# Strassen's weight sums: adding transfers on GpSimd's queue instead of VectorE additions

## The chip, the cores and the metric

The kernel runs on one core of a Trainium2 chip. A core has TensorE (matmuls; PE in the profile), VectorE (DVE), ScalarE (ACT), GpSimd (POOL) and SyncE (SP, which here only issues transfers), each with its own queue, and 16 DMA engines. The metric is the device time of one execution in microseconds. Before the change the median of 3 runs was 1128.04 us (1127.5 to 1130.51).

## The reference

Two layers over x of 512 tokens by 1024 features, all in float32. Layer 0 mixes tokens by differential attention, layer 1 by a short gated convolution; both are followed by a dense MLP:

```
def sq_relu_mlp(x, w_up, w_down):
    return jnp.square(jax.nn.relu(x @ w_up)) @ w_down

for i in range(DEPTH):
    h = rmsnorm(x, norm_mixer_pre[i])
    m = diff_attention(h, ...) if i % 2 == 0 else short_conv(h, ...)
    x = x + rmsnorm(m, norm_mixer_post[i])
    h = rmsnorm(x, norm_mlp_pre[i])
    x = x + rmsnorm(sq_relu_mlp(h, w_up[i], w_down[i]), norm_mlp_post[i])
```

w_up is 1024 x 4096, w_down 4096 x 1024.

## The kernel before, in words

**Products in three matmuls.** Every float32 operand is split into a rounded part hi and the rest lo. `split` (L199) writes hi on ScalarE (L200) and lo = operand - hi on VectorE (L201). A product of two operands is then three matmuls, hi hi, hi lo and lo hi (`mm3`, L67 to L69).

**Up projection.** The weights of the 32 feature tiles come one by one (512 KB each, `raw_up`), are split, and give 24 matmuls each into one PSUM bank. Banks 6 and 7 take turns (in a layer's first six tiles, banks 0 to 5). `squared` empties the bank on ScalarE: Relu (L674) into a scratch tile F, then Square (L675). Two feature tiles make a pair; from its F come the splits ua and ub, with differences made on VectorE (L699 to L701) in between.

**Down projection.** 28 of the 32 rows of w_down tiles are multiplied in Strassen's form (seven products instead of eight): pair p holds rows 2p and 2p + 1, each cut into two halves of 512 columns. Call the four pieces r0, r1 (row 2p) and r2, r3 (row 2p + 1). They lie in one buffer `rawd` with a fifth slot r4. The products need these operands of the weights: A = (r0, r2); E = (r0 + r1, r4) with r4 = r0 + r1 + r3; D = r3; and G = (r1 + r3, r4 + r2). So the sums are made in place: L222 adds r1 and r3 to r0 and r1 (128x1024), L223 makes r4 (128x512), L229 makes the new r2 (128x512). All three are on VectorE. A is split from the buffer before r0 and r2 are overwritten; E, D and G after their sums.

**Groups.** Two pairs (GROUP = 2) are one group: 7 groups in each layer, 14 in all, 28 buffers. A group's 84 matmuls go in the order A, E, G, D, G into banks 0 to 5; between them VectorE adds finished banks to `acc` (L724). Between two groups stand four up products (six before the last group of a layer, none before the first but the layer's first six). Four rows at the end of each layer (`raw_dn`) go without Strassen's form.

**What sets the order.** `order` lists the units: ..., up tiles, A p, A p+1, E p, E p+1, D, G p, G p+1, up tiles, ... `use` asks for the splits of a unit and of the four after it (LEAD), as far as the six slots for hi and lo (SLOTS) allow: a unit's slot is that of the unit six places before. Thus a group's A and E are split during the up products ahead of it. There are two `rawd` buffers (RAWDS), so that the next group's loads wait for the splits of G. Loads are issued by SP in the order of their use. A scheduler then fixes each engine's order; engines work their queues in order, and an instruction that waits holds those behind it.

Of the kernel before, what the change touches and what calls it, by code (L numbers as in the profile page):

```python
# [13 lines left out]
ALU = mybir.AluOpType  # L14
# [14 lines left out]
GROUP = 2  # L29
# [12 lines left out]
def trunk(ctx: ExitStack, tc: tile.TileContext, x, xT, w_qk, w_v, w_o, w_in, w_out,  # L42
          w_up, w_down, rows, cols, lam4, rope, out):
    nc = tc.nc
    PE, ACT, DVE, POOL = nc.tensor, nc.scalar, nc.vector, nc.gpsimd
# [53 lines left out]
    groups = [list(range(g, g + GROUP)) for g in range(0, PAIRED // 2, GROUP)]  # L99
# [32 lines left out]
    def loaded_by(u):  # L132

        n, i = u
        if n[0] in "AEG" and n[1:].isdigit():
            return [("rawd", n[1], i)]
        if n[0] == "D":
            return [("rawd", n[1], p) for p in groups[i]]
        return [("raw", n, i)]
# [8 lines left out]
    units, raws, xts = [], {}, []  # L148
# [15 lines left out]
    def issue():  # L164
        while n_issued[0] < len(loads):
            ld = loads[n_issued[0]]
            tag, n, i = ld
            live = in_flight[tag] = [x for x in in_flight[tag] if last_use[x] >= len(units)]
            if len(live) >= limit[tag] or tag not in allowed:
                return  # L170
            if tag == "rawd" and any(n_done[0] <= j < first_use[ld] for j in ring["rawd"]):
                return
            live.append(ld)
            first = n_issued[0] == 0
            n_issued[0] += 1
            if tag == "rawd":

                raw = raws[ld] = wp.tile([P, 5, 512], F32, tag=tag, name=f"rawd_{n}_{i}", bufs=RAWDS)
                for k in range(2):
                    nc.sync.dma_start(raw[:, 2 * k:2 * k + 2, :].rearrange("p a b -> p (a b)"), w_down[int(n), 2 * i + k])  # L180
                continue
            if n == "v":
                xt = t512(ap, f"xt_{i}", "a", RAWS)
                xts.append(xt)
            src = w_qk[2 * i + "qk".index(n)] if n in "qk" else source[n][i]
            raw = raws[ld] = wp.tile([P, 1024], F32, tag="raw", name=f"raw_{n}_{i}", bufs=RAWS)
            for p in range(2 if first else 1):
                if n == "v":
                    s = pieces(512, first)[p]
                    nc.sync.dma_start(xt[:, s], xT[i][:, s])  # L190
                s = pieces(1024, first)[p]
                nc.sync.dma_start(raw[:, s], src[:, s])
                if n == "v" and i == p == 0:
                    nc.sync.dma_start(col, cols)

    def pieces(n, cut):
        return (slice(0, n // 2), slice(n // 2, n)) if cut else (slice(0, n),)

    def split(hi, lo, src, on_dve=False):  # L199
        (DVE.tensor_copy if on_dve else ACT.copy)(hi, src)  # L200
        DVE.tensor_tensor(lo, src, hi.bitcast(F32), op=ALU.subtract)  # L201

    def make(j):
        n, i = order[j]
        if where[j][0] == "w":
            hi = wp.tile([P, 1024], F32R, tag="whi", name=f"hi_{n}_{i}")
            lo = wp.tile([P, 1024], F32R, tag="wlo", name=f"lo_{n}_{i}")
        else:
            both = wp.tile([P, 2, 1024], F32R, tag="rawd", name=f"both_{n}_{i}", bufs=RAWDS)
            hi, lo = both[:, 0, :], both[:, 1, :]  # L210
        parts = [raws[ld] for ld in loaded_by((n, i))]
        if loaded_by((n, i))[0][0] == "raw":
            if n == "v":
                split_xT(i)
            for s in pieces(1024, j < 2 or n in "qk"):
                split(hi[:, s], lo[:, s], parts[0][:, s], j < 1)
        else:
            r, (h2, l2) = parts[0], (t.rearrange("p (a b) -> p a b", a=2) for t in (hi, lo))
            if n[0] == "A":
                split(h2, l2, r[:, 0:4:2, :])  # L220
            if n[0] == "E":
                DVE.tensor_tensor(r[:, 0:2, :], r[:, 0:2, :], r[:, 1:4:2, :], op=ALU.add)  # L222
                DVE.tensor_tensor(r[:, 4, :], r[:, 0, :], r[:, 3, :], op=ALU.add)  # L223
                split(h2, l2, r[:, 0:5:4, :])
            if n[0] == "D":
                for k, p in enumerate(parts):
                    split(h2[:, k, :], l2[:, k, :], p[:, 3, :])
            if n[0] == "G":
                DVE.tensor_tensor(r[:, 2, :], r[:, 4, :], r[:, 2, :], op=ALU.add)  # L229
                split(h2, l2, r[:, 1:3, :])  # L230
        units.append((hi, lo))

    def split_to(j):
        for j_ in range(len(units), min(j + 1, len(order))):
            if where[j_][1] >= n_done[0]:
                break
            make(j_)
            issue()
# [33 lines left out]
    def split_xT(kt):  # L272

        g = g_pre[:, kt:kt + 1]
        for s in pieces(T, kt == 0):
            hi, lo = hT[0][:, kt, s], hT[1][:, kt, s]
            ACT.activation(hi, xts[kt][:, s], AF.Copy, scale=g)
            DVE.scalar_tensor_tensor(lo, xts[kt][:, s], g, hi.bitcast(F32), op0=ALU.mult, op1=ALU.subtract)
# [5 lines left out]
    def t512(pool, name, tag, bufs):  # L284
        return pool.tile([P, 512], F32, tag=tag, name=name, bufs=bufs)

    issue()
    ones = ap.tile([P, P], F32, name="ones", bufs=1)
    DVE.memset(ones, 1.0)
# [47 lines left out]
    for b in range(NB):  # L337
        for n in range(2):
            o = v_sb[:, b, n * 512:(n + 1) * 512]
# [240 lines left out]
    pool_of_chunks[:] = [(up_, CHUNKS[0])] * CHUNKS[0] + [(late, CHUNKS[1])] * CHUNKS[1]  # L580
    allowed.append("rawd")
    issue()
    x_sb = late.tile([P, NB, D], F32, name="x_sb", bufs=1)

# [301 lines left out]
```

## Time and profile before

| | |
|---|---|
| median of 3 runs | 1128.04 us |
| the profiled execution | 1127.7 us |
| its span, first to last instruction | 1125.9 us |
| TensorE busy | 1101.4 us, 98% |
| VectorE busy | 823.4 us, 73% |
| ScalarE busy | 545.2 us, 48% |
| GpSimd busy | 99.0 us, 9% |
| DMA moved | 114.31 MB, 102 GB/s in the mean |

The profile is of one execution. Busy time is the share in which an engine's instructions run. A timeline row is: start in us from the span's start, duration in us, engine, line, operation, out<-in with shapes, count of instructions that the row joins; in square brackets the idle time of the engine before it and what ended it. Matmuls are pipelined: a row's duration is longer than the distance to the next.

### The profile page before, as it was taken

The page shows a single profiled execution, that of the slowest core. Times are in us where ns is not written, and L with a number is a line of the kernel's source. Part 1 is how long each engine was busy: PE and PEld are TensorE (multiplying, and loading weights), DVE is VectorE, ACT ScalarE, POOL GpSimd, SP SyncE. Part 2 cuts the span into 40 slices and gives each one's busy share as a digit, 9 for nine tenths or more (in the row PEclk, how much of TensorE's full clock was granted, in tenths as well). Part 3 has the DMA queues.
Part 4 walks back from the last instruction along what each step waited for, and adds up shares of the span by engine and source line. Part 5 has one row for each costly group of instructions (what it writes and reads, how often), then busy time and mean ns, then how long its engine had stood idle before and what let it go on. Part 6 is the DMA issues. An engine that isn't in the chain of part 4 may idle for free.

```text
span 1125.9 us, 14245 instructions
## 1 busy us (share of the span) xinstructions
PE 1101.4 (98%) x5404; PEld 915.7 (81%) x5404; DVE 823.4 (73%) x1251; ACT 545.2 (48%) x925; POOL 99.0 (9%) x108
## 2 busy tenths in 40 slices
PE   9999999999999999999998999999999999999997
PEld 7876677778988888888887988888988888888886
DVE  5589999756788779778688544436587887797766
ACT  5546566544664544554545332224375445445532
POOL 0144455211000000000001000000000000000000
PEclk9999999999999999999998999999999999999999
DMA  8611111036134214315042322213231242242202
GB/s 311 217 57 57 57 57 53 23 113 225 38 113 150 86 65 150 104 46 188 1 150 96 130 94 94 95 55 115 93 133 64 103 150 86 65 150 99 88 20 75
DMA packets 33044, 114.31 MB, mean 102 GB/s; under 512 B 3792, under 2 KB 4432, under 8 KB 32976
## 3 DMA queue, kind: packets, MB, share of 16 engines
q1 hardware_dynamic: 32976, 113.41, 29.3%
q8 instruction: 42, 0.69, 0.2%
q14 instruction: 26, 0.21, 0.1%
HBM read 111.30 MB, written 2.10 MB: 101 GB/s over the span
## 4 chain that ended last, share of the span: by engine, by line
PE 80%; DVE 13%; POOL 3%; issue 2%; ACT 1%; DMA 1%; SPq 0%; POOLq 0%; DVEq 0%; ACTq 0%
PE bank L69 24%; PE bank L67 24%; PE bank L68 24%; PE bank L309 2%; PE pair L309 2%; DVE nm L475 2%; DVE a L500 1%; POOL t_q L375 1%; DVE k L392 1%; DVE x_sb L612 1%; DVE pair L474 1%; PE bank L629 1%; PE pair L67 1%; PE pair L69 1%; PE pair L68 1%
## 5 line engine op out<-in xcount | busy, mean ns | idle before, releaser
L67 PE MATMUL bank<-hT_hi,hi_up 128*128 128x512 f32 (+1 forms) x608 | 216.5, 356 | 0.0
L69 PE MATMUL bank<-hT_hi,lo_up 128*128 128x512 f32 (+1 forms) x608 | 216.2, 356 | 0.0
L68 PE MATMUL bank<-hT_lo,hi_up 128*128 128x512 f32 (+1 forms) x608 | 216.1, 355 | 0.0
L68 PEld LDWEIGHTS bank<-hT_lo,hi_up 128*128 128x128 f32 x608 | 114.9, 189 | 16.3
L67 PEld LDWEIGHTS bank<-hT_hi,hi_up 128*128 128x128 f32 x608 | 114.9, 189 | 16.3
L69 PEld LDWEIGHTS bank<-hT_hi,lo_up 128*128 128x128 f32 x608 | 114.9, 189 | 16.2
L724 DVE TENSOR_TENSOR acc<-acc,bank 128x512 f32<-128x512 f32 x180 | 116.5, 679 | 4.4 <-PE bank L69 4.4
L200 ACT CAST hi_up<-raw_up 128x1024 fp32r<-128x1024 f32 x64 | 67.2, 1054 | 86.9 <-PE bank L69 76.4
L201 DVE TENSOR_TENSOR lo_up<-raw_up,hi_up 128x1024 fp32r<-128x1024 f32 x64 | 76.7, 1217 | 8.8 <-ACT hi_up L200 8.8
L201 DVE TENSOR_TENSOR lo_G<-rawd,hi_G 128x1024 fp32r<-128x1024 f32 x28 | 34.2, 1220 | 44.2 <-ACT hi_G L200 44.2
L68 PE MATMUL bank<-hT_lo,hi_ci 128*128 128x512 f32 (+1 forms) x176 | 62.9, 358 | 1.8 <-DVE b_m L601 1.8
L67 PE MATMUL bank<-hT_hi,hi_ci 128*128 128x512 f32 (+1 forms) x176 | 62.8, 357 | 0.9 <-ACT hT_hi L632 0.8
L69 PE MATMUL bank<-hT_hi,lo_ci 128*128 128x512 f32 (+1 forms) x176 | 62.8, 357 | 0.0
L674 ACT ACTIVATE F<-bank 128x512 f32<-128x512 f32 x64 | 37.6, 593 | 45.3 <-PE bank L69 35.8
L200 ACT CAST hi_G<-rawd 128x1024 fp32r<-128x1024 f32 x28 | 29.5, 1053 | 46.0 <-PE bank L68 30.8
L201 DVE TENSOR_TENSOR lo_E<-rawd,hi_E 128x1024 fp32r<-128x1024 f32 x28 | 34.2, 1220 | 23.4 <-ACT hi_E L200 23.4
L201 DVE TENSOR_TENSOR lo_A<-rawd,hi_A 128x1024 fp32r<-128x1024 f32 x28 | 33.5, 1219 | 19.5 <-ACT hi_A L200 19.5
L200 ACT CAST hi_E<-rawd 128x1024 fp32r<-128x1024 f32 x28 | 29.3, 1048 | 34.8 <-PE bank L68 33.4
L200 ACT CAST hi_A<-rawd 128x1024 fp32r<-128x1024 f32 x28 | 29.5, 1053 | 30.4 <-PE bank L68 21.7
L67 PE MATMUL bank<-hi_A,ua_hi 128*128 128x512 f32 x112 | 44.0, 393 | 0.0
L68 PE MATMUL bank<-lo_A,ua_hi 128*128 128x512 f32 x112 | 43.6, 390 | 0.0
L67 PE MATMUL bank<-hi_E,ub_hi 128*128 128x512 f32 x112 | 43.6, 389 | 0.0
(300 smaller groups left out, 2661.7 us busy)
## 6 DMA issues: line engine op xcount, KB each, us to landing
raw_up<-in_w_up SPq DMA_DIRECT2D x64, 512.0 KB, 4.2
rawd<-in_w_down SPq DMA_DIRECT2D x56, 512.0 KB, 4.5
raw_ci<-in_w_in SPq DMA_DIRECT2D x24, 512.0 KB, 3.4
raw_q<-in_w_qk SPq DMA_DIRECT2D x8, 512.0 KB, 4.4
raw_k<-in_w_qk SPq DMA_DIRECT2D x8, 512.0 KB, 3.8
raw_wo<-in_w_o SPq DMA_DIRECT2D x8, 512.0 KB, 3.5
raw_dn<-in_w_down SPq DMA_DIRECT2D x8, 512.0 KB, 3.5
raw_wc<-in_w_out SPq DMA_DIRECT2D x8, 512.0 KB, 3.4
```

The source lines that it names most:

```text
L67: PE.matmul(o, lhsT=a[0], rhs=b[0], start=start, stop=False, skip_group_check=more)
L68: PE.matmul(o, lhsT=a[0], rhs=b[1], start=False, stop=False, skip_group_check=more)
L69: PE.matmul(o, lhsT=a[1], rhs=b[0], start=False, stop=stop, skip_group_check=more)
L200: (DVE.tensor_copy if on_dve else ACT.copy)(hi, src)
L201: DVE.tensor_tensor(lo, src, hi.bitcast(F32), op=ALU.subtract)
L309: PE.matmul(banks[2 * b + n], lhsT=hT[ai][:, kt, b * P:(b + 1) * P], rhs=w[bi][:, n * 512:(n + 1) * 512], start=kt == 0 and ai + bi == 0, ...
L375: POOL.tensor_tensor(t1, t1, sw, op=ALU.add)
L392: DVE.tensor_tensor(tiles[c][other], t1[mine], tiles[c][mine].bitcast(F32), op=ALU.subtract)
L474: DVE.tensor_tensor(dgl, dgl, mask.unsqueeze(1).broadcast_to([P, 2, P]), op=ALU.add)
L475: DVE.tensor_reduce(nm, s[:, :, :w], axis=AX.X, op=ALU.max, negate=True)
L674: ACT.activation(dst, o, AF.Relu)
L724: DVE.tensor_tensor(a, a, o[t], op=op)
```

## The change

The three sums leave VectorE. Each buffer gets one more plain load: r3 is also loaded into the slot r4. When A's split is emitted, `sums` emits adding transfers on GpSimd's queue (`POOL.dma_start` with `accum_op`): the transfer adds its source to what stands at the destination. First r1 and r3 are added, from DRAM, to r0 and r1 (512 KB). With the last pair of a group come two for each of its buffers, within SBUF: r0 is added to r4, and r4 to r2 (256 KB each).

```
@@ -178,6 +178,7 @@
                 raw = raws[ld] = wp.tile([P, 5, 512], F32, tag=tag, name=f"rawd_{n}_{i}", bufs=RAWDS)
                 for k in range(2):
                     nc.sync.dma_start(raw[:, 2 * k:2 * k + 2, :].rearrange("p a b -> p (a b)"), w_down[int(n), 2 * i + k])
+                nc.sync.dma_start(raw[:, 4, :], w_down[int(n), 2 * i + 1][:, 512:1024])
                 continue
@@ -199,6 +200,20 @@
+    def plus(o, a):
+        POOL.dma_start(o, a, accum_op=ALU.add)
+
+    def sums(l, p):
+        r = raws["rawd", l, p]
+        plus(r[:, 0:2, :], w_down[int(l), 2 * p:2 * p + 2, :, 512:1024].rearrange("k p c -> p k c"))
+        pq = [raws["rawd", l, x] for x in groups[p // GROUP]] if p % GROUP == GROUP - 1 else []
+        for r in pq:
+            plus(r[:, 4, :], r[:, 0, :])
+        for r in pq:
+            plus(r[:, 2, :], r[:, 4, :])
@@ -218,15 +233,13 @@
             if n[0] == "A":
                 split(h2, l2, r[:, 0:4:2, :])
+                sums(n[1], i)
             if n[0] == "E":
-                DVE.tensor_tensor(r[:, 0:2, :], r[:, 0:2, :], r[:, 1:4:2, :], op=ALU.add)
-                DVE.tensor_tensor(r[:, 4, :], r[:, 0, :], r[:, 3, :], op=ALU.add)
                 split(h2, l2, r[:, 0:5:4, :])
             if n[0] == "G":
-                DVE.tensor_tensor(r[:, 2, :], r[:, 4, :], r[:, 2, :], op=ALU.add)
                 split(h2, l2, r[:, 1:3, :])
```

GpSimd's queue at the first two groups of layer 0, in the kernel after (`rawd_0` to `rawd_3` are the buffers of pairs 0 to 3; in brackets the semaphores waited for: DMAHW of SP's transfers, DMASW of GpSimd's own):

```order
L74 TENSOR_TENSOR rb_wo_2564<-rb_wo_2564,mhalf 128x1 [waits DVE_49,Pool_49]
L205 DMA rawd_0_2589<-in_w_down 128x2x512 [waits DMAHW5_49,DVE_49]
L205 DMA rawd_1_2593<-in_w_down 128x2x512 [waits DMAHW1_49,DVE_49]
L205 DMA rawd_0_2589<-rawd_0_2589 128x512 [waits DMAHW7_49,DMASW0_49]
L205 DMA rawd_1_2593<-rawd_1_2593 128x512 [waits DMAHW3_49,DMASW1_49]
L205 DMA rawd_0_2589<-rawd_0_2589 128x512 [waits DMAHW6_49,DMASW2_49]
L205 DMA rawd_1_2593<-rawd_1_2593 128x512 [waits DMAHW2_49,DMASW3_49]
L205 DMA rawd_2_3039<-in_w_down 128x2x512 [waits DMAHW0_49,DMASW4_49,DVE_49]
```

Before, the instruction behind `rb_wo` on this queue belonged to the layer's end; now 42 adding transfers for each layer stand between them. The add into r4 waits for the first add into the same buffer, the add into r2 for the add into r4.

VectorE between the splits of A and E in a group of layer 0 (pairs 4 and 5), before:

```order
L201 TENSOR_TENSOR lo_A_4_3418<-rawd_4_3329,hi_A_4_3417 128x1024
L201 TENSOR_TENSOR lo_A_5_3449<-rawd_5_3332,hi_A_5_3448 128x1024
L222 TENSOR_TENSOR rawd_4_3329<-rawd_4_3329 128x1024
L222 TENSOR_TENSOR rawd_5_3332<-rawd_5_3332 128x1024
L223 TENSOR_TENSOR rawd_4_3329<-rawd_4_3329 128x512
L223 TENSOR_TENSOR rawd_5_3332<-rawd_5_3332 128x512
L229 TENSOR_TENSOR rawd_4_3329<-rawd_4_3329 128x512
L229 TENSOR_TENSOR rawd_5_3332<-rawd_5_3332 128x512
L201 TENSOR_TENSOR lo_E_4_3490<-rawd_4_3329,hi_E_4_3489 128x1024
```

and after (the same lines are now L202):

```order
L202 TENSOR_TENSOR lo_A_4_3424<-rawd_4_3333,hi_A_4_3423 128x1024
L202 TENSOR_TENSOR lo_A_5_3456<-rawd_5_3337,hi_A_5_3455 128x1024
L202 TENSOR_TENSOR lo_E_4_3502<-rawd_4_3333,hi_E_4_3501 128x1024
L202 TENSOR_TENSOR lo_E_5_3533<-rawd_5_3337,hi_E_5_3532 128x1024
L712 TENSOR_TENSOR F_5_3452<-F_5_3452 128x512
```

The six sums are gone, and nothing stands between the two splits.

ScalarE in the first group of layer 0 (`F_1`, `ua_1` belong to the second pair of up tiles), before:

```order
L200 CAST ua_0_hi<-F_0_2793 128x768
L200 CAST hi_E_0_2905<-rawd_0_2589 128x1024
L200 CAST ub_0_hi<-F_0_2793 128x1024
L200 CAST hi_E_1_2938<-rawd_1_2592 128x1024
L200 CAST hi_D_0_2981<-rawd_0_2589 128x512
L674 ACTIVATE F_1_2861<-bank_2577 128x2x256
L674 ACTIVATE F_1_2861<-bank_2578 128x2x256
L675 ACTIVATE F_1_2861<-F_1_2861 128x2x256 x2
L200 CAST hi_D_0_2981<-rawd_1_2592 128x512
L200 CAST ua_1_hi<-F_1_2861 128x768
```

and after:

```order
L201 CAST ua_0_hi<-F_0_2795 128x768
L201 CAST ub_0_hi<-F_0_2795 128x1024
L201 CAST hi_E_0_2913<-rawd_0_2589 128x1024
L687 ACTIVATE F_1_2864<-bank_2577 128x2x256
L687 ACTIVATE F_1_2864<-bank_2578 128x2x256
L688 ACTIVATE F_1_2864<-F_1_2864 128x2x256 x2
L201 CAST hi_E_1_2944<-rawd_1_2593 128x1024
L201 CAST ua_1_hi<-F_1_2864 128x768
```

`hi_E_0` moved behind `ub_0_hi`, `hi_E_1` behind F of the second pair; `ua_1_hi` still stands behind both.

## Rows read from the trace of the kernel before

**Rows 1.** The page: span, and busy time of each engine.

```profile
span 1125.9 us, 14245 instructions
...
PE 1101.4 (98%) x5404; PEld 915.7 (81%) x5404; DVE 823.4 (73%) x1251; ACT 545.2 (48%) x925; POOL 99.0 (9%) x108
```

**Rows 2.** Windows of one group each: length, busy PE, PEld, DVE, ACT, POOL; clock, DMA share, GB/s.

```profile
341.00:382.00 41.00, 41.00 (x183) 33.90 (x182) 32.82 (x42) 20.02 (x26) 0.00 (x0) 1.00 0.30 103
...
902.00:943.00 41.00, 41.00 (x183) 33.92 (x182) 32.80 (x42) 19.87 (x24) 0.00 (x0) 1.00 0.30 103
```

**Rows 3.** Timeline of TensorE: the first matmuls of A and of E.

```profile
381.01 0.39 PE L67 MATMUL bank<-hi_A,ua_hi 128*128 128x512 f32 x1
...
386.45 0.39 PE L67 MATMUL bank<-hi_E,ub_hi 128*128 128x512 f32 x1
```

**Rows 4.** Groups of VectorE's instructions: the three sums; count, busy us, mean ns, idle before.

```profile
L222 DVE TENSOR_TENSOR rawd<-rawd 128x1024 f32<-128x1024 f32 x28 | 33.5, 1218 | 0.2
...
L223 DVE TENSOR_TENSOR rawd<-rawd 128x512 f32<-128x512 f32 x28 | 18.5, 684 | 0.1
L229 DVE TENSOR_TENSOR rawd<-rawd 128x512 f32<-128x512 f32 x28 | 18.5, 684 | 0.1
```

**Rows 5.** Timeline of VectorE: the two splits of A in the group of rows 3.

```profile
360.38 2.35 DVE L201 TENSOR_TENSOR lo_A<-rawd,hi_A 128x1024 fp32r<-128x1024 f32 x2
```

**Rows 6.** Timeline of ScalarE, same group: splits of E, Relu of bank 7, split of G.

```profile
366.06 1.04 ACT L200 CAST hi_E<-rawd 128x1024 fp32r<-128x1024 f32 x1
370.10 1.05 ACT L200 CAST hi_E<-rawd 128x1024 fp32r<-128x1024 f32 x1 [3.01 <-PE bank L68]
371.06 0.59 ACT L674 ACTIVATE F<-bank 128x512 f32<-128x512 f32 x1
...
380.98 1.05 ACT L200 CAST hi_G<-rawd 128x1024 fp32r<-128x1024 f32 x1 [2.59 <-PE bank L68]
```

**Rows 7.** Timeline of VectorE, same group: split of G, second addition to acc (bank 1).

```profile
382.07 1.23 DVE L201 TENSOR_TENSOR lo_G<-rawd,hi_G 128x1024 fp32r<-128x1024 f32 x1 [3.82 <-ACT hi_G L200]
...
385.64 0.68 DVE L724 TENSOR_TENSOR acc<-acc,bank 128x512 f32<-128x512 f32 x1
```

**Rows 8.** The page, DMA issues: count, KB each, median us to landing.

```profile
raw_wc<-in_w_out SPq DMA_DIRECT2D x8, 512.0 KB, 3.4
...
x_sb<-in_x SPq DMA_DIRECT2D x4, 512.0 KB, 7.7
xt<-in_xT SPq DMA_DIRECT2D x7, 256.0 KB, 5.0
out_x<-x_sb SPq DMA_DIRECT2D x7, 256.0 KB, 2.0
```

**Rows 9.** The tile rawd: issues on SP; shortest, median, longest ns.

```profile
L180 SPq DMA_DIRECT2D rawd<-in_w_down x56: 327/423/1184, 260.3 to 1034.1; - x56
```

**Rows 10.** Timeline of VectorE, first group of layer 0: splits of A.

```profile
285.42 1.22 DVE L201 TENSOR_TENSOR lo_A<-rawd,hi_A 128x1024 fp32r<-128x1024 f32 x1 [3.80 <-ACT hi_A L200]
...
288.55 1.22 DVE L201 TENSOR_TENSOR lo_A<-rawd,hi_A 128x1024 fp32r<-128x1024 f32 x1
```

**Rows 11.** Timeline of ScalarE, first group of layer 0: F and ua of the second pair.

```profile
296.64 1.07 ACT L674 ACTIVATE F<-bank 128x512 f32<-128x512 f32 x2
297.60 1.15 ACT L675 ACTIVATE F<-F 128x512 f32<-128x512 f32 x2
...
299.16 0.83 ACT L200 CAST ua_hi<-F 128x768 fp32r<-128x768 f32 x1
```

**Rows 12.** Timeline of TensorE: the first matmul that reads this ua_hi.

```profile
300.05 0.49 PE L67 MATMUL bank<-hi_A,ua_hi 128*128 128x512 f32 x1
```

**Rows 13.** Windows at the end of layer 0's MLP, as in rows 2.

```profile
600.00:602.00 2.00, 0.57 (x3) 0.19 (x1) 1.87 (x4) 0.72 (x2) 0.36 (x1) 0.82 0.66 205
...
606.00:608.00 2.00, 2.00 (x12) 2.00 (x11) 1.86 (x4) 0.00 (x0) 0.00 (x0) 0.50 0.04 18
608.00:610.00 2.00, 2.00 (x19) 2.00 (x19) 0.00 (x0) 0.26 (x1) 0.55 (x1) 0.97 0.61 240
```

## The prediction

> **What bounds the kernel now.** I began with the busy time of the engines. The reader is to see there that TensorE is busy 98% of the span and VectorE 73% [rows 1]: the engine that the change relieves is not the one that fills the span. Next came the windows over the two layers' MLP, one window for each group of the down projection. TensorE is busy 41.00 of 41 us in them at full clock, VectorE about 33, ScalarE 20, and GpSimd does nothing [rows 2]. Here no VectorE time can be turned into span. The matmuls stand one behind another: from the first of A to the first of E are 24, in 386.45 - 381.01 = 5.44 us, 0.227 us each [rows 3]. Last I read the timelines of VectorE and ScalarE in one group, to find when the sums are made and how late they may be.
>
> **What goes.** The three lines of sums run 28 times each and cost 33.5 + 18.5 + 18.5 = 70.5 us of VectorE [rows 4], 5.0 us in each of the 14 groups, all beside busy matmuls. They also are all that stands between lo_A and lo_E: the two lo_A end at 360.38 + 2.35 = 362.73 and the first hi_E starts on ScalarE at 366.06 [rows 5, 6]. I cost their removal at nothing.
>
> **What comes.** Each group gets six adding transfers on GpSimd's queue: two of 512 KB from DRAM, two of 256 KB that make r4, two of 256 KB that make r2. SP gets one more plain 256 KB load for each buffer. This load and the last two adds I cost at nothing: DMA is at 0.30 in these windows [rows 2]; the load is issued with the buffer's others, long before; r2 is read first by hi_G at 380.98 [rows 6], 18 us after lo_A. GpSimd's queue has nothing else to do there, so its own waits hold nobody.
>
> The new wait is the one of hi_E, on the first four adds. It stands on ScalarE in front of the second hi_E (which starts at 370.10 when its slot is free) and of the Relu that empties bank 7 (371.06) [rows 6]; lo_E on VectorE waits with it, with the F operations behind. What is late next:
> - The Relu starts 371.06 - 370.10 = 0.96 after the second hi_E, and takes 0.59. The last up product before A, 24 matmuls, starts at 381.01 - 5.44 = 375.57 and writes that bank. So r4 of the second buffer must be there by about 375.57 - 0.96 - 0.59 = 374.0, less a short hop.
> - A delay that gets past ScalarE's 2.59 us of idle time before hi_G [rows 6] reaches VectorE's additions to acc, which stand behind lo_G and F. Bank 1 is read at 385.64 for 0.68 and written again by the fourth E matmul, at 386.45 + 3 x 0.227 = 387.13 [rows 3, 7]: 0.8 us more. That is 370.10 + 2.59 + 0.8 = 373.5.
>
> I take 373.5: 10.8 us from the end of the second lo_A. Every microsecond beyond it stops TensorE for one, once in each group.
>
> **The chain in that time** is: the two 512 KB adds, then the 256 KB add on the second buffer, which waits for its 512 KB add to land. No transfer of this trace adds, and none is issued by GpSimd, so bounds come from plain ones [rows 8]. From below, an add costs what the quickest kinds cost: 3.4 us for 512 KB and 2.0 for 256 KB, together 5.4, half the budget. From above, the crowded kinds: 7.7 and 5.0 us; if adding costs twice that, 25.4. Between them I use the quick rows with the bytes counted twice, since an add must read its destination as well: 3.4 - 2.0 = 1.4 us for each further 256 KB gives 3.4 + 2 x 1.4 = 6.2 for the first kind and 2.0 + 1.4 = 3.4 for the second. Two large adds at once share the engines, so the second lands 2.8 us behind the first. For issuing I take what SP's issue of a rawd load takes, 0.42 us in the median [rows 9], twice in the chain, and keep the shortest and longest of these, 0.33 and 1.18, as its ends. Then: first lo_A ends about 361.6; its add lands at 361.6 + 0.4 + 6.2 = 368.2, the second at 371.0, the r4 add at 371.0 + 0.4 + 3.4 = 374.8. That is 1.3 us too late.
>
> The Trainium skill has a price for transfers from GpSimd's queue: "DMA: Bandwidth & Descriptors", section "Anatomy of one DMA — SWDGE (gpsimd) path", gives about 2.0 us plus bytes over 436 GB/s, that is an estimate of 3.2 us for 512 KB and 2.6 for 256 KB. It is stated for plain transfers and no run here shows it. By it the chain ends near 370 and nothing is late: the first rival below.
>
> **The sum.** Of the 14 groups, the first of each layer is of another kind (below). In the last of each layer the same lines stand further apart (six up products are between, not four), and I cost it at nothing. Ten groups remain: 10 x 1.3 = 13 us.
>
> First group: the two lo_A end at 285.42 + 1.22 = 286.64 and 288.55 + 1.22 = 289.77 [rows 10]. By the same prices the large adds land at 293.2 and 296.4, the r4 adds at 297.0 and 300.2. ScalarE now has hi_E of buffer 0, then F of the second pair (about 2.1 us, 296.64 to 298.75 before), then hi_E of buffer 1, then ua_hi [rows 11]: 297.0 to 298.1, to 300.2, to 301.2, to 302.05. Before, ua_hi ended at 299.99, and the matmul that reads it ran at 300.05, at once [rows 11, 12]. So TensorE waits 2.1 us, in two layers 4.2.
>
> 13 + 4.2 = 17.2 us on the profiled execution's 1127.7 gives 1145 us; that execution lies 0.3 us under the median of the runs shown, 1128.04. I put no clock loss into it, but the range holds one: where TensorE was busy for only 0.57 of the 2 us from 600, its granted clock fell, and it still stood at 0.50 (1.2 GHz) from 606 to 608 [rows 13]. Some 6 us at half speed lose 3 us of work. Waits of 1.3 us, 41 us apart, may stay under that; waits over 2 us may not.
>
> **Rivals.**
> 1. The chain is hidden, and the time stays. The adds take about what plain transfers take; r4 is there before 373.5 and, in the first groups, before 298. For it: DMA at 0.30, an idle queue, 5.0 us less on VectorE in front of lo_E. Against: two transfers in series replace 1.22 + 0.68 = 1.90 us of VectorE. Time 1127.5 to 1131. By the price of the Trainium skill given above it would be 1128.
> 2. The adds are heavy. Each large add costs the crowded 7.7 us, its pair 2.8 more, the second kind 5.4 with its issue: 361.6 + 0.4 + 7.7 + 2.8 + 5.4 + 0.4 = 378.3, 4.8 us late. With the lost clock 4.8 + 3 = 7.8 us in ten groups, and about 5.5 + 3 in each first group (ua_hi then ends near 305.5): 78 + 17 = 95, to 1223. It decides from a chain of some 13 us on. For it: an adding transfer does a read, an add and a write for each piece, and two of 512 KB come at once. Against: 16 engines with 70% of their time free.
> 3. Faster. VectorE's relief would have to reach the places where TensorE does wait: 1125.9 - 1101.4 = 24.5 us in all [rows 1]. Those I looked at (the attention, the ends of the layers, the last block) hold none of the removed lines. Only another order of neighbours at the layers' seams could move a microsecond or two: 1122 to 1124.
>
> **Chances.** The forecast's case (waits of some tenths to 3 us a group: 1132 to 1170) 0.42; hidden 0.29; heavy 0.24; faster 0.05. What differs by under 0.3% (3.4 us) can't be told from no change here. So slower 0.42 + 0.24 = 0.66, same 0.29, faster 0.05. The range is 1126 to 1215 us: it holds the hidden case, the forecast's and the lower part of the heavy one; the forecast's own range is 1132 to 1170.
>
> **What would show it.** In the profile after: VectorE's busy time lower by 70 us; no sums among its lines. hi_E's idle time before it put down to the adding transfer, 4 us or more in a usual group, and the chain from the second lo_A to the landing of the r4 add near 12 us; a time from issue to landing of about 6 us for the large adds and 3.4 for the small ones. TensorE's waits then name bank 7's Relu or the acc additions, 1.3 us in each of ten groups, and ua_hi in the first group of each layer. I am wrong if TensorE's windows stay at 41.00 of 41 (rival 1), or if the granted clock falls in every group (rival 2). If hi_E is not held by the transfers at all and the time still moves, the whole reading is wrong.

## The result, and the profile after

| | before | after |
|---|---|---|
| median of the device time, us | 1127.8 (4 runs) | 1209.4 (1207.4 to 1211.7, 4 runs) |
| ratio to before | | 1.0725, 95% interval 1.0709 to 1.0741 |
| span of the profiled execution, us | 1125.9 | 1205.7 |
| TensorE busy, us | 1101.4 | 1131.0 |
| VectorE busy, us | 823.4 | 759.8 |

The change costs 81.6 us. The forecast was 1145, so its sign was right and its size a fifth of what came; the time is inside the range on record, in the part that had been taken in for rival 2.

The page of the changed kernel answers to [rows 1, 8]: span, busy time, the share of GpSimd's DMA queue, and the issues of the adding transfers with their median time to landing.

```profile
span 1205.7 us, 14473 instructions
...
PE 1131.0 (94%) x5404; PEld 934.8 (78%) x5404; DVE 759.8 (63%) x1167; ACT 546.4 (45%) x925; POOL 183.4 (15%) x192
...
q0 software_dynamic: 15680, 29.37, 14.7%
...
rawd<-in_w_down POOLq DMA_DIRECT2D x28, 512.0 KB, 5.9
rawd<-rawd POOLq DMA_DIRECT2D x56, 256.0 KB, 3.4
```

VectorE lost 63.6 us of work, where the prediction had 70, and TensorE did not get them: its busy time grew by 29.6 us and its idle time by 50.2 (1205.7 - 1131.0 = 74.7, against 24.5). The adding transfers land in 5.9 and 3.4 us; the prediction had 6.2 and 3.4.

TensorE's waits (engine, line, what for, us in total, times, longest) hold nearly the whole of the idle part in two lines; neither is among TensorE's waits in the kernel before. L687 is the Relu that empties bank 7 (L674 before), L201 ScalarE's half of `split` (L200 before).

```profile
PE bank L67 <- ACT F L687: 40.7, 10, 6.0
PE bank L67 <- ACT ua_hi L201: 10.0, 2, 5.1
```

Ten waits of 4.1 us on the Relu, one in each of ten groups, and one of 5 us on ua_hi in the first group of each layer: the places that the prediction named, at two to three times the size. The other 29.6 us, in which TensorE counts as busy, are nearly all slow clock: windows of 1 us over the whole span, busy time times what the granted clock lacks of 1.00, add up to 32.4 us here and to 4.5 in the kernel before, an estimate of 27.9 us. Windows of TensorE over one usual group of the changed kernel (length, busy time, granted clock, DMA share, GB/s), to be read beside [rows 2]:

```profile
389.00:391.00 2.00, 2.00 (x9) 1.00 0.48 85
391.00:393.00 2.00, 0.03 (x1) 1.00 0.90 153
393.00:395.00 2.00, 0.25 (x1) 1.00 0.74 128
395.00:397.00 2.00, 2.00 (x8) 0.72 0.68 117
397.00:399.00 2.00, 2.00 (x6) 0.50 0.04 8
399.00:401.00 2.00, 2.00 (x9) 0.93 0.00 0
```

TensorE stands still for 3.7 us and then works for some 4 us at a granted clock that falls to 0.50 (1.2 GHz). Behind the stop, "busy" is not "at speed": 6 matmuls in two microseconds where there were 9 or 10.

GpSimd's timeline in the same group shows why r4 is late (start, duration, instruction, idle time before it and what ended it):

```profile
377.33 1.22 POOL L205 DMA_DIRECT2D rawd<-in_w_down  x1 [29.27 <-DVE lo_A L202]
383.47 1.23 POOL L205 DMA_DIRECT2D rawd<-in_w_down  x1 [4.93 <-issue]
384.21 1.43 POOL L205 DMA_DIRECT2D rawd<-rawd  x1
389.79 0.86 POOL L205 DMA_DIRECT2D rawd<-rawd  x1 [4.14 <-DMA rawd<-in_w_down]
391.00 0.86 POOL L205 DMA_DIRECT2D rawd<-rawd  x1 [0.35 <-DMA rawd<-rawd]
393.45 0.86 POOL L205 DMA_DIRECT2D rawd<-rawd  x1 [1.58 <-DMA rawd<-rawd]
```

Both lo_A are done at 375.68 + 2.36 = 378.04 (next fence), but the second large add is issued at 383.47, 6.1 us behind the first, when that one has landed. The row's releaser is "issue": no semaphore of the program held it. The r4 add of the second buffer follows at 389.79, when the second large add has landed. It is so in twelve of the 14 groups: the lines of this transfer over the whole span (count, busy us, mean ns, idle before), first in this kernel, then in e5_room_1536 below, where GpSimd has more room, are

```profile
L205 POOL DMA_DIRECT2D rawd<-in_w_down x28 | 34.9, 1246 | 450.3 <-DVE lo_A L202 338.9 <-issue 61.0 <-DMA raw_up<-in_w_up 50.4
...
L205 POOL DMA_DIRECT2D rawd<-in_w_down x28 | 35.1, 1274 | 384.2 <-DVE lo_A L202 332.4 <-DMA raw_up<-in_w_up 51.8
```

61.0 us of "issue", and none. VectorE's row and ScalarE's rows of the group around 380, to be read beside [rows 5, 6]:

```profile
375.68 2.36 DVE L202 TENSOR_TENSOR lo_A<-rawd,hi_A 128x1024 fp32r<-128x1024 f32 x2
```

```profile
390.75 1.04 ACT L201 CAST hi_E<-rawd 128x1024 fp32r<-128x1024 f32 x1 [9.30 <-DMA rawd<-rawd]
393.15 1.04 ACT L201 CAST hi_E<-rawd 128x1024 fp32r<-128x1024 f32 x1 [1.35 <-DVE lo_E L202]
394.10 0.59 ACT L687 ACTIVATE F<-bank 128x512 f32<-128x512 f32 x1
```

From the end of the second lo_A to the second hi_E are 393.15 - 378.04 = 15.1 us. The row of the second hi_E names lo_E of the first buffer, which ended just then; but the r2 add of the second buffer at 393.45, in GpSimd's rows above, waited until then for the same r4 add to land. The prediction had 12.1 for this chain and 10.8 for its budget.

### The profile page after: what moved, and what is told of

It reads as the page before. It is cut to its first block, busy times and chain, and to the rows that moved or that the text cites. A ratio compares the mean times of both kernels' runs of the same rounds, so it can differ in the third digit from the quotient of the medians.

```text
span 1205.7 us, 14473 instructions
## 1 busy us (share of the span) xinstructions
PE 1131.0 (94%) x5404; PEld 934.8 (78%) x5404; DVE 759.8 (63%) x1167; ACT 546.4 (45%) x925; POOL 183.4 (15%) x192
## 3 DMA queue, kind: packets, MB, share of 16 engines
q0 software_dynamic: 15680, 29.37, 14.7%
## 4 chain that ended last, share of the span: by engine, by line
PE 41%; issue 26%; DVE 14%; DMA 8%; POOL 6%; ACT 4%; POOLq 0%; ACTq 0%; DVEq 0%; SPq 0%
PE bank L67 12%; PE bank L68 11%; PE bank L69 11%; DMA rawd<-rawd 4%; DMA rawd<-in_w_down 3%; POOL rawd L205 3%; PE bank L322 2%; PE pair L322 2%; DVE nm L488 1%; DVE a L513 1%; ACT hi_E L201 1%; POOL t_q L388 1%; DVE x_sb L625 1%; DVE lo_G L202 1%; DVE k L405 1%
## 5 line engine op out<-in xcount | busy, mean ns | idle before, releaser
L67 PE MATMUL bank<-hT_hi,hi_up 128*128 128x512 f32 (+1 forms) x608 | 227.0, 373 | 40.7 <-ACT F L687 40.7
L68 PE MATMUL bank<-hT_lo,hi_up 128*128 128x512 f32 (+1 forms) x608 | 224.2, 369 | 0.0
L69 PE MATMUL bank<-hT_hi,lo_up 128*128 128x512 f32 (+1 forms) x608 | 224.0, 368 | 0.0
L67 PEld LDWEIGHTS bank<-hT_hi,hi_up 128*128 128x128 f32 x608 | 120.1, 198 | 62.8 <-ACT F L687 44.9
L202 DVE TENSOR_TENSOR lo_E<-rawd,hi_E 128x1024 fp32r<-128x1024 f32 x28 | 34.3, 1225 | 177.2 <-ACT hi_E L201 177.2
L68 PEld LDWEIGHTS bank<-hT_lo,hi_up 128*128 128x128 f32 x608 | 120.4, 198 | 17.7
L69 PEld LDWEIGHTS bank<-hT_hi,lo_up 128*128 128x128 f32 x608 | 119.6, 197 | 18.3
L201 ACT CAST hi_up<-raw_up 128x1024 fp32r<-128x1024 f32 x64 | 67.3, 1055 | 86.1 <-PE bank L69 76.7
L205 POOL DMA_DIRECT2D rawd<-in_w_down x28 | 34.9, 1246 | 450.3 <-DVE lo_A L202 338.9
L201 ACT CAST hi_E<-rawd 128x1024 fp32r<-128x1024 f32 x28 | 29.3, 1045 | 136.8 <-DMA rawd<-rawd 134.2
L202 DVE TENSOR_TENSOR lo_up<-raw_up,hi_up 128x1024 fp32r<-128x1024 f32 x64 | 76.8, 1220 | 9.0 <-ACT hi_up L201 8.8
L205 POOL DMA_DIRECT2D rawd<-rawd x56 | 55.4, 989 | 97.3 <-DMA rawd<-in_w_down 64.5
L687 ACT ACTIVATE F<-bank 128x512 f32<-128x512 f32 x64 | 37.6, 594 | 45.9 <-PE bank L69 37.4
L202 DVE TENSOR_TENSOR lo_A<-rawd,hi_A 128x1024 fp32r<-128x1024 f32 x28 | 33.5, 1222 | 29.5 <-ACT hi_A L201 29.5
L202 DVE TENSOR_TENSOR lo_G<-rawd,hi_G 128x1024 fp32r<-128x1024 f32 x28 | 34.2, 1222 | 25.6 <-ACT hi_G L201 25.6
L69 PE MATMUL bank<-hi_A,ua_lo 128*128 128x512 f32 x112 | 44.9, 401 | 0.6 <-DVE ua_lo L202 0.6
```

The costliest lines, as they stand in the source:

```text
L67: PE.matmul(o, lhsT=a[0], rhs=b[0], start=start, stop=False, skip_group_check=more)
L68: PE.matmul(o, lhsT=a[0], rhs=b[1], start=False, stop=False, skip_group_check=more)
L69: PE.matmul(o, lhsT=a[1], rhs=b[0], start=False, stop=stop, skip_group_check=more)
L205: POOL.dma_start(o, a, accum_op=ALU.add)
L687: ACT.activation(dst, o, AF.Relu)
```

## The experiments

The theory after the result: GpSimd's room for descriptors (1024 bytes a partition in this kernel) does not hold two 512 KB adds, so the second waits until the first has landed; that makes the chain 15.1 us where it should be near 12, and the slow clock follows the longer stops. Rivals: the adds are heavy in themselves; added DMA traffic disturbs the loads; GpSimd's queue is slow whatever it carries; the lost sums changed the order elsewhere.

All ratios are to runs of the kernel before on the same chip.

| run | median us | ratio, 95% interval |
|---|---|---|
| e1_ring | 1158.8 | 1.0267, 1.0244 to 1.0291 |
| e2_no_sums | 1126.8 | 0.9997, 0.9984 to 1.0010 |
| e3_halves | 1140.7 | 1.0113, 1.0095 to 1.0130 |
| e4_early | 1207.2 | 1.0690, 1.0659 to 1.0720 |
| e5_room_1536 | 1157.9 | 1.0263, 1.0245 to 1.0281 |
| e6_plain | 1133.1 | 1.0049, 1.0031 to 1.0066 |
| e7_r2_only | 1128.2 | 1.0001, 0.9990 to 1.0011 |
| e8_halves_late | 1133.3 | 1.0044, 1.0027 to 1.0060 |
| e9_halves_five | 1130.1 | 1.0016, 1.0005 to 1.0027 |

### Room for two large adds (e1_ring)

```
-        return st.tile([P, n], F32, tag=f"st{n}", name=name, bufs=12)
+        return st.tile([P, n], F32, tag=f"st{n}", name=name, bufs=12 if n < 4 else 2)
-    nc = bacc.Bacc("TRN2", ..., dynamic_dma_scratch_size=1024)
+    nc = bacc.Bacc("TRN2", ..., dynamic_dma_scratch_size=2048)
```

> The changed kernel with twice the SBUF room for the descriptors of GpSimd's transfers (2048 bytes a partition in place of 1024; to make room, the four-wide small tiles have 2 buffers in place of 12). In the changed kernel GpSimd's second large add is issued 4.9 us after the first one's issue ended, with nothing that it visibly waits for. Theory (no room for the descriptors of two large adds at once): the second is issued some 1.3 us after the first, the two share the engines, the r4 add of the second buffer lands about 12 us after the second lo_A in place of 15; TensorE waits about 1 to 2 us a group in place of 4, with less time at half clock; 1140 to 1165 us. Rival (GpSimd waits for something else between two adds, for instance each add is worked off before the next is written): the 4.9 us stay, about 1209 us.

50 of the 81.6 us are gone. GpSimd's timeline in one usual group of this run:

```profile
374.35 2.46 POOL L205 DMA_DIRECT2D rawd<-in_w_down  x2 [29.31 <-DVE lo_A L202]
```

Both large adds are issued back to back, and the chain from lo_A to the second hi_E is 386.61 - 375.13 = 11.5 us. TensorE's waits on the Relu fall from ten of 4.1 us to four of 5.0 us in all. What is left in a usual group shows only at the weight loads (PEld), because the matmuls already under way cover the rest of it:

```profile
388.20 0.19 PEld L67 LDWEIGHTS bank<-hT_hi,hi_up 128*128 128x128 f32 x1 [0.49 <-ACT F L687]
400.18 0.19 PEld L67 LDWEIGHTS bank<-hi_E,ub_hi 128*128 128x128 f32 x1 [0.54 <-DVE acc L737]
```

These are the two deadlines of the prediction, the Relu of bank 7 and the additions to acc, one after the other, and the clock stays at 1.00.

### The same with nothing else touched (e5_room_1536)

```
-    nc = bacc.Bacc("TRN2", ..., dynamic_dma_scratch_size=1024)
+    nc = bacc.Bacc("TRN2", ..., dynamic_dma_scratch_size=1536)
```

> The changed kernel with one number altered: the room in which GpSimd writes descriptors is 1536 bytes a partition instead of 1024 (2048 was tried together with fewer buffers for some small tiles; here nothing else is touched). Theory (room by bytes moved): in the changed kernel a 256 KB add was issued while the second 512 KB add was still under way, so 1024 holds at least 768 KB of adds and fewer than two large ones; 1536 then holds 1152 KB or more, both large adds are issued back to back, the chain ends as it did with 2048 and the time is 1154 to 1164 us. Rival 1 (one large add takes a whole share of 1024, whatever its bytes): nothing changes, 1209 us. Rival 2 (with 2048 it was the smaller tile buffers that helped): nothing changes either, 1209 us.

1157.9 us: half as much room again does what twice as much does, and the smaller buffers of e1_ring had no part in it. GpSimd's rows in one usual group of this run, the large adds and the two r4 adds:

```profile
370.02 2.48 POOL L205 DMA_DIRECT2D rawd<-in_w_down  x2 [28.88 <-DVE lo_A L202]
376.43 0.90 POOL L205 DMA_DIRECT2D rawd<-rawd  x1 [3.93 <-DMA rawd<-in_w_down]
378.97 0.86 POOL L205 DMA_DIRECT2D rawd<-rawd  x1 [1.63 <-DMA rawd<-in_w_down]
```

The second large add does not need the first to have landed. What it waits for in the changed kernel is room, which comes free when the first lands.

### The adding itself (e6_plain)

```
     def plus(o, a):
-        POOL.dma_start(o, a, accum_op=ALU.add)
+        POOL.dma_start(o, a)
```

> The changed kernel with the adding taken out of its GpSimd transfers: same sizes, same queue, same order, same waits, but each overwrites instead of adding, so the sums are not computed. Theory A (it is the adding that costs: read, add, write): plain transfers of 512 KB land in 3.4 to 4.4 us and 256 KB in 2.0 to 2.6 instead of 5.9 and 3.4; the second large one is still issued only when the first has landed; the chain from the second lo_A to r4 falls from 15.1 to about 10.8 us, and the time is 1130 to 1150 us. Theory B (it is GpSimd's queue, whatever it carries): 5.9 and 3.4 us again, 1209 us.

1133.1 us: same queue, sizes, order and semaphores, 76 us less. (The kernel leaves the sums out.) The rows of this run's page, to be read beside those of the changed kernel above:

```profile
q0 software_dynamic: 8512, 29.37, 7.4%
...
rawd<-in_w_down POOLq DMA_DIRECT2D x28, 512.0 KB, 4.1
rawd<-rawd POOLq DMA_DIRECT2D x56, 256.0 KB, 2.3
```

So adding costs 1.8 us on 512 KB and 1.1 on 256 KB in the median; with two large adds under way at once, as here, e5_room_1536 has 6.2 us for 512 KB. The bytes are the same 29.37 MB, but the adding ones go in 15680 packets instead of 8512 and take 14.7% of the engines' time instead of 7.4%. GpSimd is quicker at issuing them too, and here the second large transfer does not wait for the first, although the room is 1024 (groups of instructions: count, busy us, mean ns, idle before; then one usual group):

```profile
L205 POOL DMA_DIRECT2D rawd<-rawd x56 | 30.8, 551 | 86.1 <-DMA rawd<-in_w_down 60.6 <-DMA rawd<-rawd 23.3 <-issue 2.0
L205 POOL DMA_DIRECT2D rawd<-in_w_down x28 | 20.5, 732 | 408.2 <-DVE lo_A L202 381.0 <-DMA raw_up<-in_w_up 27.2
```

```profile
364.57 0.71 POOL L205 DMA_DIRECT2D rawd<-in_w_down  x1 [29.15 <-DVE lo_A L202]
365.71 0.73 POOL L205 DMA_DIRECT2D rawd<-in_w_down  x1 [0.43 <-DVE lo_A L202]
```

I had expected the second to wait here as well; it does not, which fits a time at the lower end. It fits a room that is filled by packets. The run e7_r2_only below has 28 adding transfers of 256 KB and no others on this queue:

```profile
q0 software_dynamic: 4032, 7.34, 3.8%
```

That is 144 packets each. If all the small adds of the changed kernel go so, 15680 - 56 x 144 = 7616 are left for its 28 large ones, 272 each. Two large adds are then 544 packets and do not fit in 1024; a large and a small one (416) do, as the row at 384.21 above shows, and two plain large ones (304, at the mean of this run, 8512 / 112 = 76 for each 256 KB) do. That it is packets that are counted was not tried by itself; e4_early below gives two more points.

### No sums at all (e2_no_sums)

```
-                DVE.tensor_tensor(r[:, 0:2, :], r[:, 0:2, :], r[:, 1:4:2, :], op=ALU.add)
-                DVE.tensor_tensor(r[:, 4, :], r[:, 0, :], r[:, 3, :], op=ALU.add)
-                split(h2, l2, r[:, 0:5:4, :])
+                split(h2, l2, r[:, 0:4:3, :])
...
-                DVE.tensor_tensor(r[:, 2, :], r[:, 4, :], r[:, 2, :], op=ALU.add)
```

> The kernel before with the three sums of the weights left out (E is split from r0 and r3, G from r1 and r2 as loaded), so the result is not the reference's. It takes all that the change could take off VectorE, 70 us of busy time, and adds nothing. Theory (TensorE fills these stages; VectorE's time is worth nothing there): 1126 to 1129 us, TensorE's windows at 41.00 of 41. Rival (the relief of VectorE is worth something and the change's waits hide it): 1060 to 1120 us.

0.9997: to be rid of the sums at no price at all gains nothing that can be measured. The windows of [rows 2] in this run (same columns), VectorE at 28.40 instead of 32.8:

```profile
341.00:382.00 41.00, 41.00 (x183) 33.92 (x182) 28.40 (x37) 20.05 (x25) 0.00 (x0) 1.00 0.30 104
```

TensorE fills the window with and without them. VectorE's busy time over the span is 759.2 us, 64.2 less than before. Another place for these sums has no more than this to win from VectorE, 0.16% by the interval.

### Smaller adds, one done ahead (e3_halves)

```
                 nc.sync.dma_start(raw[:, 4, :], w_down[int(n), 2 * i + 1][:, 512:1024])
+                POOL.dma_start(raw[:, 1, :], w_down[int(n), 2 * i + 1][:, 512:1024], accum_op=ALU.add)
...
-        plus(r[:, 0:2, :], w_down[int(l), 2 * p:2 * p + 2, :, 512:1024].rearrange("k p c -> p k c"))
+        plus(r[:, 0, :], w_down[int(l), 2 * p][:, 512:1024])
```

> The changed kernel with the large add cut in two 256 KB adds: r3 is added to r1 right after the load (no split reads r1 as loaded), r1 to r0 after A's split as now; the sums are the same. So only one 256 KB add and the r4 add stand between lo_A and hi_E. Theory (the length of the chain sets the wait): the chain is 0.9 + 3.4 + 0.9 + 3.4 us and about 1 for sharing, 9 to 10 us, inside the 10.8 us that the trace of before allows: no waits in the ten usual groups, at most 1 us in the first groups, 1128 to 1133 us. Rival (any adding transfer between A and E costs, for instance since descriptors have no room): 1150 us or more.

1140.7, above what I expected. In the usual groups it does as expected, the chain being 377.38 - 367.84 = 9.5 us and TensorE without a wait; what is left is in the first two groups of each layer, and 0.7 us in the last (table below).

### All adds that can be early, early (e4_early)

```
                 nc.sync.dma_start(raw[:, 4, :], w_down[int(n), 2 * i + 1][:, 512:1024])
+                for o, s in ((4, w_down[int(n), 2 * i][:, 0:512]), (1, w_down[int(n), 2 * i + 1][:, 512:1024]), (4, w_down[int(n), 2 * i][:, 512:1024])):
+                    POOL.dma_start(raw[:, o, :], s, accum_op=ALU.add)
...
-        plus(r[:, 0:2, :], w_down[int(l), 2 * p:2 * p + 2, :, 512:1024].rearrange("k p c -> p k c"))
...
-        for r in pq:
-            plus(r[:, 4, :], r[:, 0, :])
+        plus(raws["rawd", l, p][:, 0, :], w_down[int(l), 2 * p][:, 512:1024])
```

> The changed kernel with r4 built by two adds from DRAM right after the load (r0 and r1 onto the copy of r3), r1 likewise; after A's split only r0's add (256 KB) and r2's stand. All sums are still made by adding transfers, with 256 KB more of them from DRAM for each buffer. Theory (the wait comes from the chain, not from the number of adds or the bytes): one add stands before hi_E, about 5 us, hidden; 1127 to 1130 us, like before and not faster. Rival (the adds cost by their number or bytes, through DMA or GpSimd's queue): 1150 us or more.

A clear miss: 1207.2, no better than the change itself, with twelve waits of 4.4 us on the Relu. GpSimd's timeline in one usual group of this run (L183 are the early adds, L207 those after A):

```profile
371.18 1.79 POOL L183 DMA_DIRECT2D rawd<-in_w_down  x2 [7.74 <-DMA rawd<-in_w_down]
374.35 0.86 POOL L183 DMA_DIRECT2D rawd<-in_w_down  x1 [1.37 <-DMA rawd<-in_w_down]
381.25 0.86 POOL L183 DMA_DIRECT2D rawd<-in_w_down  x1 [6.05 <-DMA rawd<-in_w_down]
381.79 1.24 POOL L207 DMA_DIRECT2D rawd<-in_w_down  x1
```

The early adds are not early, and they are slow. The chain of work that ended last, in the same stretch, shows it (start, length, what):

```profile
364.89 9.06 DMA rawd<-in_w_down
...
374.35 6.51 DMA rawd<-in_w_down
...
381.25 0.54 POOL rawd L183
381.79 5.74 DMA rawd<-in_w_down
```

The last load of the second buffer, issued when the group before is done with it, lands at 373.95 after 9.06 us; the add that follows takes 6.51 us and the one behind A 5.74, where e3_halves has 5.1 in the median for 256 KB from DRAM. GpSimd's queue is in order, so the adds after A stand behind the early ones until 381.79. I had counted their durations and not what they stand in front of. The rival (the adds cost by their number or bytes) may be right in part: this queue carries 36.71 MB in place of 29.37, and the page has SP's loads of r4 at 7.2 us to landing and those of raw_up at 6.4, where the changed kernel has 4.7 and 4.2. How much of the miss is order and how much is traffic was not separated.

Descriptor room shows again behind these rows:

```profile
382.42 1.51 POOL L207 DMA_DIRECT2D rawd<-rawd  x1
385.61 0.86 POOL L207 DMA_DIRECT2D rawd<-in_w_down  x1 [1.68 <-issue]
387.84 0.86 POOL L207 DMA_DIRECT2D rawd<-rawd  x1 [1.37 <-issue]
```

The adds at 381.25, 381.79 and 382.42 go out one behind the other, and the fourth waits 1.7 us with "issue" as its releaser. By 144 packets each, three are 432 and four 576: with the sums above, 1024 bytes would hold 432 packets and not 544.

### Only the sum that nobody waits for (e7_r2_only)

```
                 DVE.tensor_tensor(r[:, 4, :], r[:, 0, :], r[:, 3, :], op=ALU.add)
+                POOL.dma_start(r[:, 2, :], r[:, 4, :], accum_op=ALU.add)
...
-                DVE.tensor_tensor(r[:, 2, :], r[:, 4, :], r[:, 2, :], op=ALU.add)
```

> The kernel before with only one of the three sums moved: r2 += r4 becomes a 256 KB adding transfer, issued right after VectorE has made r4; r0, r1 and r4 stay on VectorE. Theory (only the chain that hi_E waits for costs; r2 is read by hi_G more than 10 us later, and this add takes about 4.5 us with its issue): no wait, 1126 to 1130 us, VectorE's busy time 18.5 us less. Rival (28 adding transfers disturb the loads or the engines by themselves): 1135 us or more.

1.0001: 28 adding transfers with 10 us to spare cost nothing, and VectorE's 15.6 us less (807.8 against 823.4) are worth nothing. This much adding traffic, a quarter of the change's bytes, does not slow the kernel.

### Adding transfers in five of seven groups (e8_halves_late, e9_halves_five)

As e3_halves, with VectorE's sums in the first two groups of each layer (the three lines with `if i < 2 * GROUP:` ahead). In e8 the first two sums stand right after A's split and the third after E's:

> The version with 256 KB adds and one of them done ahead (1140.7 us), but with the sums of the first two groups of each layer back on VectorE; the other five groups of each layer keep their adding transfers. Theory (its 13 us are all in the first two groups of each layer, where lo_A stands close before the first E product; by the starts of hi_G 4.9 us in layer 0 and 4.0 in layer 1, and 1 to 2 after them): 1126 to 1131 us. Rival (they are spread over the groups, or come from the added DMA traffic): 1135 to 1141 us.

1133.3, a miss by 2 us. By the starts of hi_G the five later groups of a layer cost nothing but 0.5 us in the last, and about 2 us came in behind the first group of each layer, where nothing adds by transfer any more. The sums' own place had changed there. So e9 puts them where the kernel before has them:

> As the run before it (256 KB adds in the last five groups of each layer, VectorE's sums in the first two), but in the first two groups the three sums stand where the kernel before has them, r2's ahead of hi_G and the others ahead of hi_E; there they stood ahead of hi_E's neighbours, the r2 sum ahead of ub_lo, and hi_G came to stand ahead of ua_hi. Theory (the 5.9 us that were left came from that other order in the first group of each layer, about 2 us each by the starts of hi_G, and nothing from the adding transfers): 1126 to 1130 us, no change. Rival (the adding transfers of the five groups cost the rest): 1132 to 1135 us as before.

1130.1, 1.0016: the 2 us are gone. By the interval, 1.0005 to 1.0027, ten groups with adding transfers cost some 0.6 to 3 us in all.

### The groups side by side

The first hi_G of a group starts on ScalarE at a fixed place of the program. Its start minus the start in the kernel before, taken from group to group, is what each group lost (us; seven groups of layer 0, then seven of layer 1). Two such rows of the changed kernel:

```profile
355.46 1.05 ACT L201 CAST hi_G<-rawd 128x1024 fp32r<-128x1024 f32 x1 [0.23 <-PE bank L68]
...
401.90 1.05 ACT L201 CAST hi_G<-rawd 128x1024 fp32r<-128x1024 f32 x1 [0.45 <-PE bank L68]
```

In the kernel before the second of them starts at 380.98 [rows 6], and the first here:

```profile
340.14 1.05 ACT L200 CAST hi_G<-rawd 128x1024 fp32r<-128x1024 f32 x1 [2.58 <-PE bank L68]
```

That is 46.44 us against 40.84, 5.6 us lost. The last column is the chain in the group around 380, from the end of the second lo_A to the second hi_E.

| run | layer 0 | layer 1 | chain |
|---|---|---|---|
| after | 6.6, 8.7, 5.6, 6.7, 5.2, 5.6, 0.0 | 5.5, 8.3, 6.7, 6.4, 7.0, 6.8, 0.0 | 15.1 |
| e5_room_1536 | 3.2, 4.9, 1.5, 2.2, 1.5, 2.4, -0.1 | 4.1, 4.1, 1.5, 1.3, 1.5, 1.4, -0.1 | 11.6 |
| e3_halves | 3.4, 1.4, -0.1, 0.0, 0.0, 0.0, 0.7 | 1.7, 2.3, -0.1, 0.0, 0.0, 0.0, 0.7 | 9.5 |
| e6_plain | 2.2, 0.5, -0.1, 0.0, 0.0, 0.0, 0.0 | 1.2, 0.7, -0.1, 0.0, 0.0, 0.0, 0.0 | 8.6 |

The first number of each layer also holds what the layer's other stages moved by (e2_no_sums, where nothing can wait for a sum, has -1.7 and -3.5 there). The table is a curve of loss against the chain's length: none at 8.6 and 9.5 us, 1.5 at 11.6, 5.2 to 7.0 at 15.1. The budget lies near 10 us (an estimate, 11.6 - 1.5 = 10.1), where the prediction had 10.8. From 11.6 to 15.1 us the loss grows by 3.7 to 5.5 us for 3.5 us of chain, since the slow clock is added.

## Why the prediction was wrong

**Right.** VectorE's time in these groups is worth nothing (e2_no_sums, e7_r2_only). The new wait is the one of hi_E, behind it the Relu of bank 7 and acc; the tenfold wait, the last group of each layer at nothing, and ua_hi in the first group: all as named. The prices of the adds, taken from quick plain rows with the bytes counted twice, came out: 6.2 and 3.4 us forecast, 5.9 and 3.4 measured, and e6_plain shows that it is the adding that doubles the engines' time. That they came out so near is partly luck: plain transfers on this queue take 4.1 and 2.3 us, not 3.4 and 2.0, and adding puts 1.8 and 1.1 on top, not 2.8 and 1.4. The estimate of 3.2 and 2.6 us by the Trainium skill, in "DMA: Bandwidth & Descriptors", section "Anatomy of one DMA — SWDGE (gpsimd) path", is short of what an adding transfer takes in this trace; for plain transfers on this queue e6_plain measures 4.1 and 2.3.

**The step that failed** is "Two large adds at once share the engines, so the second lands 2.8 us behind the first." They never run at once. In a usual group the second is issued 6.1 us behind the first, for want of descriptor room. With room (e5_room_1536) that step is right: GpSimd issues the r4 adds 378.97 - 376.43 = 2.5 us apart, as the large ones land, and a usual group loses 1.3 to 2.4 us where 1.3 were forecast. The failed step is 1209.4 - 1157.9 = 51.5 of the 81.6 us, and it brought the second error with it: no clock loss was put into the sum, because waits of 1.3 us were expected. With room the clock indeed stayed at 1.00 in all ten groups; without, it fell to 0.50 in every one, the sign that the prediction had set down for rival 2, and some 28 us are lost to it in all. The ten groups priced at 13 us cost 67.0 by the table.

**A term too small.** The second group of each layer was counted as a usual one. It is not. In the kernel before, the second lo_A there ends at 324.85 and the Relu of bank 7 follows at 330.22, 5.4 us later, where a usual group has 371.06 - 362.73 = 8.3 [rows 5, 6]:

```profile
323.63 1.22 DVE L201 TENSOR_TENSOR lo_A<-rawd,hi_A 128x1024 fp32r<-128x1024 f32 x1
```

```profile
330.22 0.59 ACT L674 ACTIVATE F<-bank 128x512 f32<-128x512 f32 x1
```

That is 3 us less to spare, a budget of 7.8 us in place of 10.8, and by the prediction's own chain of 12.1 us it would be 4.3 us late and not 1.3. The runs bear it out. In the second group of layer 0 the chain, from the end of the second lo_A to the second hi_E, is 16.2 us after the change, 12.6 in e5_room_1536, 9.7 in e3_halves and 8.2 in e6_plain; the loss is 8.7, 4.9, 1.4 and 0.5, near the chain less 7.8. I had read one group and multiplied by ten.

The first groups, priced at 2.1 us each, cost 6.6 and 5.5, and 3.2 and 4.1 with room. Their wait on ua_hi alone is 5.0 us each without room and 2.5 with it (4.9 in the two), so this term was near right but for the failed step; what else these groups lose was not separated from the other order of the stages ahead of them. Of the 30 us that are left with room, the first groups are 7.3, the second 9.0 and the eight usual ones 13.3.

**Two smaller errors with little effect.** An issue of 0.42 us was put ahead of each add. The time to landing already counts from the start of the issue (the first large add above starts at 377.33, and at 383.47 it has landed, 6.1 us later, with 5.9 the median), so it is in it; GpSimd takes 1.25 us for a large add and 0.87 to 0.99 for a small one. And the 70.5 us of VectorE are a sum of lines whose instructions overlap at their ends: without the sums VectorE is busy 64.2 us less (e2_no_sums). To cost the load of r4 and the r2 adds at nothing was right.

**The rivals.** Rival 2, "the adds are heavy", forecast 7.8 us in ten groups, 4.8 of lateness and 3 of clock; measured are 6.7, some 4 and 2.6. Its size was nearly right by luck and its reason wrong: of the 28 large adds one took 7.9 us, the others 6.5 or less. (Its sum also counts one issue of 0.4 too many: 377.9, 4.4 us late.) Rival 1 needed a chain under the budget; it is nearly what e6_plain shows, at the plain prices. No version here beats the kernel before, and by e2_no_sums there is next to nothing to win.

## What to carry to other kernels

When transfers are queued one behind the other on one engine, ask what the second needs besides free DMA engines: here it was descriptor space, and the row that shows it is an idle queue whose releaser is "issue". Before an engine is relieved, take its work out altogether and time that (0.9997 here): it bounds what can be gained. And a slack read in one group of a loop holds for the groups that have the same neighbours; look at the first two as well.

## What the runs showed of the hardware that was not expected

- An adding transfer on GpSimd's queue goes in 140 packets on average for each 256 KB where a plain one has 76 (144 for a small add by itself, in e7_r2_only), takes twice the share of the engines (14.7% and 7.4%), and costs GpSimd 1.25 us to issue for 512 KB instead of 0.73.
- With 1024 bytes a partition for descriptors a second 512 KB add is held back 4.9 us; with 1536 or 2048 it is not. Two plain 512 KB transfers fit in 1024, three adds of 256 KB do, and a fourth waits 1.7 us (e4_early).
- After TensorE stood still for 3.7 us, its granted clock was 0.72, then 0.50 (1.2 GHz), then 0.93 in the next three windows of 2 us; after waits of about 0.5 us at the weight loads it stayed at 1.00.
